# Where the halves of weight chunks land: five places in place of two from the second layer's feed-forward on

## The chip, the cores and the metric

The kernel runs on one core of one Trainium2 chip. The metric is the device time of one execution in microseconds. The kernel before took 1754.6 us (median of 3 runs, 1752.81 to 1756.55). Two runs are told apart here only when they differ by more than about 0.2%, which is 3.5 us.

## The reference

The work is four transformer layers, one after the other, on 256 tokens of width 1024 in f32, with a second stream of 256 context tokens in the first layers.

```python
# layers 0, 1 (first_block)
x = x + g1 * (concat([out_a, out_b, out_c]) @ w_out[i])       # three mixers
x = x + g2 * conv_ffn(modulate(rms_norm(x, n2g), sh2, sc2), w_up[i], conv_w[i], conv_b[i], w_down[i])
# layers 2, 3 (second_block): attention, then a pooling mixer
x = x + gate_m * rmsnorm(y, g_post_mix[i])
x = x + gate_f * rmsnorm(conv_ffn_2(...), g_post_ffn[i])

def conv_ffn(h, w_up, conv_w, conv_b, w_down):
    a = conv3(h @ w_up) + conv_b          # a depthwise convolution over 3 tokens
    gate, val = split(a)                  # in layers 2, 3 only the gate is convolved
    return (silu(gate) * val) @ w_down    # w_up is 1024 x 5632, w_down 2816 x 1024
```

Shift, scale and gate (the modulation) come from one vector per stream, multiplied with a weight of 1024 x 6144 for each layer.

## The kernel before, in words

Every weight matrix is read once, as a list of chunks of up to 128 x 2048 f32 (1 MB), in the order in which they are used (`make_plan`). A chunk passes through two stages:

- **Raw.** `fetch` (L203) issues its load on SP's queue. Most chunks come as two halves of 512 KB (L222 to L224), each into one of two places of the tag `w`. A chunk for which `roomy` (L198) holds comes whole (L219) into one of the seven large rooms of the tag `x8`; such chunks are about every third one of a feed-forward, and not the first ones of it.
- **Parts.** The same function then splits the chunk, in pieces of 384 columns: ACT rounds it to the upper part (`wh`, L238) and DVE subtracts that from the raw piece (`wl`, L240). A place of `w` is free again when the last `wl` piece of its half is done. The parts stand in two rooms of each of the tags `wh` and `wl`, or, for every third chunk, in `x8`.

`weights` (L246) is called by each unit of work on TensorE. For chunk i it has chunks up to i+2 loaded and up to i+1 split (one more where chunk i+2 is roomy). A feed-forward unit `up` is 48 matmuls in groups of 24: the upper part with both parts of h, and the lower part with the upper one (L285, L286, L289). Then ACT and DVE take the result out of PSUM (the tag S, two places): L988, L991 and L993 are the convolution, L1021 the silu, L1024 and L1026 the product, L1028 and L1029 its parts. A unit `down` ends on DVE in L980 (layer 1) or L1051 (layers 2 and 3).

TensorE's instructions and SP's DMA issues stand in program order (`manual_schedule`, L1370). SP waits for nothing but a free place, so it runs ahead of TensorE as far as places allow, and each load waits behind all those ahead of it. ACT's and DVE's instructions are put in order at build time by the scheduler, by its own estimate of when each could start and of the places that are free; on the chip each engine then runs its list in that order.

The modulation has its own loads. `mod_load` (L362) takes a chunk either whole into `x8` or as two halves into the three places of the tag `mw` (L372). The second way is used while the mixers of layers 0 and 1 run (`fill_a`, L955); L410 multiplies with them. From layer 1's feed-forward on, modulation loads go into `x8` (L366).

The stages of the profile are: layer 1's feed-forward (about 925 to 1145 us), layer 2's attention (to 1298), its feed-forward (to 1500), layer 3's pooling mixer (to 1548), its feed-forward (to the end).

Of the kernel before, what the change touches and what calls it, by code (L numbers as in the profile page):

```python
# [11 lines left out]
F32 = mybir.dt.float32  # L12
# [7 lines left out]
P = 128  # L20
# [6 lines left out]
CH = 2048  # L27
# [78 lines left out]
class Stack:  # L106
# [25 lines left out]
    def make_plan(self):  # L132
        plan = []

        def add(name, off, n, extra, cut=None):
            plan.append((name, off, n, extra, cut or n // 2))

        for i in range(4):
            T = 512 if i == 0 else 256
            if i < 2:  # L140
                for c in range(8):
                    add((f"win{i}", c), c * P * CH, CH, False)
                for c in range(4):
                    add((f"wout{i}", c), c * P * CH, CH, c > 1)
                if i == 1:
                    add(("wqkv/c", 0), 0, CH, True)
            elif i == 2:
                for c in range(6):
                    add(("wqkv", c), c * P * CH, CH, False)
                for c in range(4):  # L150
                    add(("wo", c), c * P * CH, CH, True)
            else:
                add(("wpool", 0), 0, CH, True)
            cols = 512 if T == 512 else 256
            off = 0
            for kind, g, j in self.ffn_order(T):
                gk = FF_GROUPS[T][g]
                if kind == "up":
                    add((f"wup{i}", j), j * P * CH, CH, True)
                else:  # L160
                    for c in range(D // cols):
                        add((f"wdn{i}", g, c), off, gk * cols, True, (gk + 1) // 2 * cols)
                        off += P * gk * cols
            if i == 1:
                add(("wqkv/c", 1), P * CH, CH, True)
        base = 1
        for n, (name, off, size, extra, cut) in enumerate(plan):
            if name[0][:3] == "wup" and name[1] == 0:
                base = n + 2
            elif n == 0 or name == ("wo", 0):  # L170
                base = 1 if n == 0 else n + 1
            plan[n] = name, off, size, extra and (n - base) % 3 == 0, cut
        self.plan = plan
        self.early = {}
        n = [p[0] for p in plan].index(("wup2", 0))
        self.early[n - 2] = self.early[n - 1] = n + 1
        self.pos = {p[0]: i for i, p in enumerate(plan)}
        self.raws, self.parts, self.n_whole = [], [], 0

    @staticmethod  # L180
    def ffn_order(T):
# [16 lines left out]
    def roomy(self, n):  # L198
        name, _, _, extra, _ = self.plan[n]
        return (extra and name[0][:3] in ("wup", "wdn") and int(name[0][3]) >= 1 and  # L200
                (name[1] >= 3 if name[0][:3] == "wup" else name[1] < 2))

    def fetch(self, raws, parts):  # L203


        while len(self.raws) < min(raws, len(self.plan)):
            i = len(self.raws)
            (key, *_), off, n, _, c = self.plan[i]
            src = self.a[key.split("/")[0]][off:off + P * n].rearrange("(p n) -> p n", p=P)
            if key in WHOLE:  # L210
                self.n_whole += 1
                w = self.wp.tile([P, CH], F32, tag=("wh", "wl")[self.n_whole % 2], name="ww")
                self.nc.sync.dma_start(out=w[:, :n], in_=src)
                self.raws.append(w)
                continue
            halves = []
            if self.roomy(i):
                w = self.x8("w")
                self.nc.sync.dma_start(out=w[:, :n], in_=src)  # L219
                self.raws.append([w[:, :c], w[:, c:]])  # L220
                continue
            for a, b in ((0, c), (c, n)):  # L222
                w = self.wp.tile([P, CH // 2], F32, tag="w", name="w", bufs=2)
                self.nc.sync.dma_start(out=w[:, :b - a], in_=src[:, a:b])  # L224
                halves.append(w)
            self.raws.append(halves)
        while len(self.parts) < min(parts, len(self.plan)):
            i = len(self.parts)
            (key, *_), _, n, _, c = self.plan[i]
            if key in WHOLE:  # L230
                self.parts.append((self.raws[i],))
                self.raws[i] = None
                continue
            h, l = self.wtile("wh", i), self.wtile("wl", i)
            for (a, b), w in zip(((0, c), (c, n)), self.raws[i]):
                for c in range(a, b, SPLIT):
                    d = min(b, c + SPLIT)
                    self.nc.scalar.copy(h[:, c:d], w[:, c - a:d - a])  # L238
                    with self.tc.issue_after(self.gate[0]) if self.gate and self.gate[1] == 0 else nullcontext():
                        self.nc.vector.tensor_tensor(l[:, c:d], w[:, c - a:d - a], h[:, c:d].bitcast(F32), ALU.subtract)  # L240
            if self.gate:
                self.gate = (self.gate[0], self.gate[1] - 1) if self.gate[1] else None
            self.raws[i] = None
            self.parts.append((h, l))
# [1378 lines left out]
```

## Time and profile before

| | |
|---|---|
| median of 3 runs | 1754.6 us |
| the profiled execution | 1753.49 us, span 1751.7 us, mean granted TensorE clock 0.966 |
| TensorE matmul busy | 1603.6 us (92% of the span), x12604 |
| TensorE weight loads busy | 1419.0 us (81%) |
| DVE busy | 1191.0 us (68%) |
| ACT busy | 880.2 us (50%) |
| DMA | 288.36 MB, mean 165 GB/s |
| chain that ended last | PE 65%, DVE 18%, DMA 8%, ACT 6% |

Busy shares are means over stages with different limits. Lines of TensorE's timeline carry in brackets the idle time ahead of an instruction and what ended it. A matmul is shown with a duration of 0.28 us at the full clock, and such matmuls follow each other at 0.12 us, because they overlap.

### The profile page before, as it was taken

What the parts mean: (1) busy time and instruction counts of PE and PEld (TensorE: products, weight loads), DVE (VectorE), ACT (ScalarE), POOL (GpSimd) and SP (SyncE); (2) the same over time, 40 slices, a digit from 0 to 9 for tenths busy, and PEclk for the clock granted to TensorE, in tenths of its full rate; (3) what the DMA queues carried; (4) which work ended last, traced back from release to release, by engine and by line L of the source; (5) the groups of instructions that cost most, each with busy time, mean ns of one, the idle gap of its engine ahead of it and who ended that gap; (6) DMA issues with size and microseconds to landing.
All of it is one profiled execution on the core that took longest, in us unless ns stands there. A gap on an engine that the chain in (4) does not pass through costs nothing.

```text
span 1751.7 us, 32328 instructions
## 1 busy us (share of the span) xinstructions
PE 1603.6 (92%) x12604; PEld 1419.0 (81%) x12604; DVE 1191.0 (68%) x2879; ACT 880.2 (50%) x2145; POOL 131.6 (8%) x160
## 2 busy tenths in 40 slices
PE   7999887999999999889789899988979999779997
PEld 5878456989898989787468899976759999579996
DVE  5865786755554645787788778785676567876665
ACT  5443644533243423455646656563556565656663
POOL 0000000000000000010000101000141012330110
PEclk9999798999999999999999999998989999889999
DMA  8344331345545454434434454565545546435552
GB/s 312 121 145 145 125 96 61 145 152 191 225 152 221 152 189 168 168 121 132 148 119 145 177 190 140 175 213 209 196 174 172 194 162 225 176 118 198 169 178 88
DMA packets 67403, 288.36 MB, mean 165 GB/s; under 512 B 7729, under 2 KB 9009, under 8 KB 54961
## 3 DMA queue, kind: packets, MB, share of 16 engines
q1 hardware_dynamic: 65664, 283.91, 46.0%
q10 hardware_dynamic: 1584, 2.38, 0.5%
q8 instruction: 99, 1.62, 0.4%
q14 instruction: 56, 0.45, 0.1%
HBM read 285.21 MB, written 1.05 MB: 163 GB/s over the span
## 4 chain that ended last, share of the span: by engine, by line
PE 65%; DVE 18%; DMA 8%; ACT 6%; issue 2%; POOL 0%; SPq 0%; ACTq 0%; DVEq 0%; POOLq 0%
PE S L285 10%; PE S L286 10%; PE S L289 9%; PE acc L285 9%; PE acc L286 8%; PE acc L289 8%; DVE wl L240 5%; PE acc L410 3%; DMA w<-in_wup_dram 3%; ACT wh L238 2%; DMA w<-in_wdn_dram 2%; DVE ht L529 2%; DVE mx L661 1%; PE tr L671 1%; DMA wm<-in_wmod_dram 1%
## 5 line engine op out<-in xcount | busy, mean ns | idle before, releaser
L240 DVE TENSOR_TENSOR wl<-w,wh 128x384 fp32r<-128x384 f32 (+2 forms) x1010 | 489.9, 524 | 216.3 <-ACT wh L238 204.6
L238 ACT CAST wh<-w 128x384 fp32r<-128x384 f32 (+2 forms) x1010 | 422.3, 477 | 323.1 <-DMA w<-in_wup_dram 86.2
L285 PE MATMUL S<-hH,wh 128*128 128x256 f32 x1408 | 351.0, 286 | 28.5 <-ACT hH L539 17.4
L286 PE MATMUL S<-hL,wh 128*128 128x256 f32 x1408 | 349.1, 285 | 4.7 <-POOL hL L537 4.0
L285 PEld LDWEIGHTS S<-hH,wh 128*128 128x128 f32 x1408 | 271.6, 193 | 33.8 <-ACT hH L539 18.1
L286 PEld LDWEIGHTS S<-hL,wh 128*128 128x128 f32 x1408 | 271.4, 193 | 7.1 <-POOL hL L537 5.0
L285 PE MATMUL acc<-gH,wh 128*128 128x256 f32 (+1 forms) x728 | 208.8, 311 | 8.4 <-DVE xc L980 4.8
L286 PE MATMUL acc<-gL,wh 128*128 128x256 f32 (+1 forms) x728 | 205.3, 306 | 0.0
L289 PE MATMUL S<-hH,wl 128*128 128x256 f32 x1408 | 198.3, 284 | 0.0
L289 PEld LDWEIGHTS S<-hH,wl 128*128 128x128 f32 x1408 | 182.5, 193 | 0.0
L285 PEld LDWEIGHTS acc<-gH,wh 128*128 128x128 f32 x728 | 138.8, 191 | 22.5 <-issue 7.5
L289 PE MATMUL acc<-gH,wl 128*128 128x256 f32 (+1 forms) x728 | 145.6, 306 | 0.0
L286 PEld LDWEIGHTS acc<-gL,wh 128*128 128x128 f32 x728 | 138.9, 191 | 5.5
L991 DVE SCALAR_TENSOR_TENSOR cgv<-S,sm,cgv 128x255 f32<-128x255 f32 (+1 forms) x132 | 74.9, 568 | 67.6 <-ACT cgv L988 66.8
L289 PEld LDWEIGHTS acc<-gH,wl 128*128 128x128 f32 x728 | 110.1, 191 | 6.5
L988 ACT ACTIVATE cgv<-S,sm 128x256 f32<-128x256 f32 (+1 forms) x132 | 83.1, 630 | 47.7 <-PE S L289 47.6
L285 PE MATMUL acc<-wh,hH 128*128 128x256 f32 x344 | 90.6, 295 | 10.1 <-ACT hH L539 7.9
L1029 POOL TENSOR_TENSOR gL<-cgv,gH 128x256 fp32r<-128x256 f32 x66 | 52.2, 791 | 573.9 <-ACT gH L1028 552.7
L980 DVE SCALAR_TENSOR_TENSOR x<-acc,mod,x 128x256 f32<-128x256 f32 x104 | 50.0, 482 | 56.8 <-PE acc L289 56.3
L286 PE MATMUL acc<-wl,hH 128*128 128x256 f32 x344 | 87.5, 286 | 0.0
L286 PE MATMUL S<-hcL,wh 128*128 128x256 f32 x352 | 86.5, 284 | 0.3 <-DVE hcL L540 0.3
L285 PE MATMUL S<-hcH,wh 128*128 128x256 f32 x352 | 86.4, 281 | 0.0
(268 smaller groups left out, 2839.0 us busy)
## 6 DMA issues: line engine op xcount, KB each, us to landing
wm<-in_wmod_dram SPq DMA_DIRECT2D x72, 1024.0 KB, 7.6
w<-in_wup_dram SPq DMA_DIRECT2D x140, 512.0 KB, 4.0
w<-in_wdn_dram SPq DMA_DIRECT2D x56, 512.0 KB, 4.0
mw<-in_wmod_dram SPq DMA_DIRECT2D x48, 512.0 KB, 4.6
w<-in_wup_dram SPq DMA_DIRECT2D x18, 1024.0 KB, 7.1
w<-in_win_dram SPq DMA_DIRECT2D x32, 512.0 KB, 4.1
w<-in_wout_dram SPq DMA_DIRECT2D x16, 512.0 KB, 4.8
w<-in_wqkv_dram SPq DMA_DIRECT2D x16, 512.0 KB, 3.8
```

The source lines that it names most:

```text
L238: self.nc.scalar.copy(h[:, c:d], w[:, c - a:d - a])
L240: self.nc.vector.tensor_tensor(l[:, c:d], w[:, c - a:d - a], h[:, c:d].bitcast(F32), ALU.subtract)
L285: mm(o, lhsT=s[0], rhs=m[0], start=k == ks[0], stop=False)
L286: mm(o, lhsT=s[0], rhs=m[1], start=False, stop=False)
L289: mm(o, lhsT=S(b, k)[1], rhs=M(b, k)[0], start=False, stop=end and k == ks[-1])
L410: nc.tensor.matmul(acc[32 * u:32 * u + 32], lhsT=self.cpad[:, k], rhs=w[:, 256 * u:256 * u + 256], start=k == ks[0], stop=k == ks[-1])
L529: nc.vector.scalar_tensor_tensor(t, self.xs[s][:, ft], A, r, ALU.mult, ALU.mult)
L661: nc.vector.tensor_reduce(mx, S[:, :, :nk], AX.X, ALU.max)
L980: self.nc.vector.scalar_tensor_tensor(x, acc[:, c], self.mods(i, j)[:, ft, s:s + 1], x, ALU.mult, ALU.add)
L988: nc.scalar.activation(out, ps, AF.Identity, scale=cw[:, n + f:n + f + 1], bias=cb[:, f:f + 1])
L991: nc.vector.scalar_tensor_tensor(o[:, :, 1:256], x[:, :, 0:255], cw[:, f:f + 1], o[:, :, 1:256], ALU.mult, ALU.add)
L1029: (nc.vector if T == 512 else nc.gpsimd).tensor_tensor(gL[:, a], c[:, 1, :T], gH[:, a].bitcast(F32), ALU.subtract)
```

## The change

From the chunk `("wup1", 0)` on, the halves go in turn into five places: two of the tag `w`, and three of the tag `mw`, in the order mw, w, mw, mw, w. Earlier halves go to `w` as before. Nothing else is edited: which chunks are loaded whole, the order of the loads on SP, the number of rooms for the parts and the memory in use stay as they are.

```diff
-        self.raws, self.parts, self.n_whole = [], [], 0
+        self.raws, self.parts, self.n_whole, self.n_half = [], [], 0, 0
...
+    def raw_half(self, n):
+
+        self.n_half += n >= self.pos["wup1", 0]
+        if self.n_half % 5 in (0, 2):
+            return self.wp.tile([P, CH // 2], F32, tag="w", name="w", bufs=2)
+        return self.mp.tile([P, 1024], F32, tag="mw", name="w", bufs=3)
...
             for a, b in ((0, c), (c, n)):
-                w = self.wp.tile([P, CH // 2], F32, tag="w", name="w", bufs=2)
+                w = self.raw_half(i)
                 self.nc.sync.dma_start(out=w[:, :b - a], in_=src[:, a:b])
```

## Rows read from the trace of the kernel before

**Rows 1.** View by stretches, three feed-forwards; busy us and count by engine, clock, DMA share, GB/s

```profile
925.00:1145.00 220.00, 207.02 (x1677) 203.61 (x1676) 170.06 (x385) 130.29 (x320) 18.79 (x22) 0.98 0.50 168
...
1298.00:1500.00 202.00, 193.72 (x1628) 188.62 (x1628) 133.79 (x300) 119.21 (x293) 34.33 (x44) 0.99 0.56 191
...
1548.00:1742.00 194.00, 189.35 (x1573) 187.89 (x1572) 119.97 (x277) 113.73 (x274) 17.92 (x25) 1.00 0.48 163
```

**Rows 2.** What TensorE waited for, 925 to 1100: total us, times, longest us

```profile
PE S L285 <- DVE cgv L993: 4.8, 7, 1.5
PE S L285 <- ACT wh L238: 4.1, 2, 3.6
PE acc L285 <- DVE x L980: 1.9, 1, 1.9
```

**Rows 3.** What SP's queue waited for, 920 to 1145

```profile
SPq L224 <- DVE wl L240: 159.3, 50, 17.9
...
SPq L219 <- PE S L286: 0.6, 2, 0.3
```

**Rows 4.** SP's timeline at the start of layer 1's feed-forward: start us, us, issue

```profile
905.24 0.33 SPq L224 DMA_DIRECT2D w<-in_wup_dram  x1
...
925.01 14.67 SPq L224 DMA_DIRECT2D w<-in_wup_dram  x4
```

**Rows 5.** Chain of waits, 925 to 975: start us, us, what

```profile
937.41 3.81 DMA w<-in_wup_dram
...
953.53 4.74 DMA w<-in_wup_dram
```

**Rows 6.** TensorE's timeline, 961 to 978: start us, us, instruction, count, idle before

```profile
961.86 1.12 PE L289 MATMUL S<-hH,wl 128*128 128x256 f32 x8
966.56 0.55 PE L285 MATMUL S<-hH,wh 128*128 128x256 f32 x1 [3.58 <-ACT wh L238]
...
971.82 0.41 PE L285 MATMUL S<-hH,wh 128*128 128x256 f32 x1
...
974.83 0.28 PE L285 MATMUL S<-hH,wh 128*128 128x256 f32 x1
```

**Rows 7.** TensorE's timeline, last use of a modulation place in the mixers

```profile
905.08 1.07 PE L410 MATMUL acc<-mw,cpad 128*32 128x256 f32 x16
```

**Rows 8.** Chain of waits, 975 to 1150

```profile
1060.02 8.57 DMA w<-in_wup_dram
```

**Rows 9.** DVE's timeline, 974 to 1003

```profile
980.82 2.39 DVE L240 TENSOR_TENSOR wl<-w,wh 128x384 fp32r<-128x384 f32 x5 [0.42 <-ACT wh L238]
```

**Rows 10.** TensorE's timeline, the wait behind that row

```profile
987.13 0.35 PE L285 MATMUL S<-hH,wh 128*128 128x256 f32 x1 [0.62 <-DVE cgv L993]
```

**Rows 11.** What TensorE waited for, layers 2 and 3's feed-forwards

```profile
PE acc L285 <- DVE y L1051: 1.4, 3, 0.6
PE S L285 <- DVE cgv L1026: 0.9, 1, 0.9
...
PE S L285 <- DVE cgv L1026: 1.0, 1, 1.0
```

**Rows 12.** SP's timeline in layer 2's attention

```profile
1172.70 1.60 SPq L224 DMA_DIRECT2D w<-in_wqkv_dram  x2
1174.35 4.49 SPq L366 DMA_DIRECT2D wm<-in_wmod_dram  x4
```

**Rows 13.** TensorE's timeline in the same place

```profile
1182.68 1.07 PE L410 MATMUL acc<-wm,cpad 128*32 128x256 f32 x16 [1.88 <-DMA wm<-in_wmod_dram]
1185.09 1.94 PE L410 MATMUL acc<-wm,cpad 128*32 128x256 f32 x16 [1.34 <-DMA wm<-in_wmod_dram]
```

**Rows 14.** View by stretches around it, TensorE alone

```profile
1185.00:1195.00 10.00, 9.60 (x66) 0.72 1.01 417
```

**Rows 15.** ACT's timeline at the end of the attention

```profile
1276.49 0.51 ACT L238 CAST wh<-w 128x384 fp32r<-128x384 f32 x1 [2.03 <-DMA w<-in_wup_dram]
```

**Rows 16.** DMA issues of the page: KB each, median us from issue to landing

```profile
w<-in_wup_dram SPq DMA_DIRECT2D x140, 512.0 KB, 4.0
```

## The prediction

> **What bounds the kernel now.** I read the view by stretches first, to see which stage has anything to give. In the three feed-forwards that the change reaches, matmuls fill 207.0 of 220, 193.7 of 202 and 189.4 of 194 us at a clock of 0.98 to 1.00 [rows 1]. So TensorE is the bound there, and only its gaps can be won. [...]
>
> Next, the waits of TensorE, because they say who makes the gaps. In layer 1's feed-forward it waits 4.1 us for ACT's split (longest 3.6), 4.8 us in seven waits for the convolution to free a place of S, and 1.9 us for DVE's update of x [rows 2]. Layers 2 and 3 have only 1.4, 0.9 and 1.0 us of this kind [rows 11].
>
> Then SP's queue, to see why a split is late. SP stands 159.3 us of this stage in front of L224 until a `wl` piece frees a half's place, and only 0.6 us in front of L219 for a large room [rows 3]. Loads are held up by the two places, not by `x8` or by the DMA engines (busy share 0.50 [rows 1]). Last the chain: at the start of the stage it runs from a load to a split to the next load, over and over [rows 5].
>
> **Part A, the start of layer 1's feed-forward.** The chunks up 0 to up 4 are not roomy, so ten halves in a row go through two places. The second half is issued at 905.24, the next only at 925.01, when the first split has freed a place [rows 4]. From there each half costs a landing of 3.8 to 4.7 us and a split before the place is free again [rows 5]. Up 5, which is roomy, is queued behind all ten. TensorE is done with up 4 at 962.98 and starts up 5 at 966.56, after 3.58 idle [rows 6].
>
> With five places, half n waits for half n-5. The three `mw` places were last read by the matmuls that end at 905.08 + 1.07 = 906.15 [rows 7], so this new wait is over before anyone needs the data. Behind it on SP stand only further halves of the same layer, since the loads of the mixers come earlier in the order. Five halves are 2.6 MB; at even 168 GB/s, the mean of the stage [rows 1], they take 15.6 us and have landed near 922, before the first split frees anything (925.01 [rows 4]). The last of ten halves then waits for the fifth half's split, not the eighth's. Three halves are 1.5 chunks, and a chunk is 48 matmuls at 0.12 us, 5.76: both it and up 5 move about 8.6 us forward. That covers 3.58 us.
>
> The gap also cost clock. The first 24 matmuls behind it take from 966.56 to 971.82, 5.26 us, the next 24 to 974.83, 3.01 [rows 6]; at 0.12 us each, the spacing at 2.4 GHz, 24 take 2.88. Lost: 2.4 + 0.1 = 2.5 us. The other wait for a split is 4.1 - 3.6 = 0.5 us [rows 2]. A is 3.6 + 2.5 + 0.5 = **6.6 us**, and I take it whole: 8.6 is over twice the gap.
>
> **Part B, the waits for PSUM and for x in the rest of that stage.** They have two origins. One is a late large load: SP can issue it only behind two halves, at 1060.02, and it lands 8.57 us later [rows 8]; ACT, which runs its list in order, stands in front of it while the convolution's pieces behind it grow late, and so does the place of S. More places take that away. The other is a burst: five `wl` pieces in 2.39 us without a wait among them [rows 9], with TensorE's 0.62 us behind them [rows 10]. More places do nothing for it, and may make bursts commoner, as loaded halves are ready together. Bounds: all of 4.8 + 1.9 = 6.7 us [rows 2], or none and 0.62 for every third of 22 chunks, 7 x 0.62 = 4.3 us lost. I take **3.5 us**, about half, as the long waits are of the first kind.
>
> **Part C, layers 2 and 3's feed-forwards.** 1.4 + 0.9 + 1.0 = 3.3 us are open [rows 11]. Bounds 0 and 3.3; I take **1.5**.
>
> **Part D, layer 2's attention.** Four modulation loads stand behind the halves of `wqkv` on SP: the halves are issued at 1172.70, the loads at once behind them at 1174.35 [rows 12]. TensorE waits 1.88 and 1.34 us for them [rows 13], and the clock in the next 10 us is 0.72 [rows 14]. If 1 is 2.4 GHz and 0.5 is 1.2, the half rate held for (1 - 0.72) / 0.5 = 56% of it, and cost half of that, 2.8 us. Halves that wait for the fifth-last place move these loads forward by about a chunk and a half, at the pace of this stage's splits more than the 3.2 us missing. Gain 0 (if the large rooms are not free earlier) to 3.2 + 2.8 = 6.0; I take **3**, as the rooms can't be seen.
>
> **Part E, the handovers between stages.** At the end of the attention ACT stands 2.03 us in front of a half of `wup2` [rows 15], with the norm's rstd behind it. An earlier half removes up to that; but a split that is ready earlier can also be put ahead of the norm's steps on DVE. Bounds: 2.0 gained, or at each of four handovers a whole chunk's six pieces at 2.39 / 5 = 0.48 us [rows 9], 4 x 2.9 = 11.5 lost. I take **0.4 us**, near the seen row.
>
> No work is added: issues, pieces and bytes are as before.
>
> **Sum.** 6.6 + 3.5 + 1.5 + 3 + 0.4 = 15.0 us, from the profiled execution's 1753.49 us (span 1751.7 and 1.8 around it): 1738.5. That execution lies 1.1 below the median of 1754.6, so against the runs I say **1739.5 us**.
>
> **Rivals.**
>
> 1. *Only the start is mended.* A holds, the rest is bursts and DVE's own load (170 of 220 us busy in layer 1 [rows 1]). 1754.6 - 6.6 = **1748**. For it: the 0.62 behind a burst. Against: the load that lands 8.57 us after a late issue.
>
> 2. *Nothing changes.* Halves get places, and SP then stands in front of the large rooms, so loads start as before, **1754.6**. For it: L219 is in the same queue. Against: only 0.6 us of waiting there in layer 1 [rows 3]; only a part of the halves' 159.3 would have to move there, though.
>
> 3. *Slower: the splits move ahead of the critical steps on DVE.* The scheduler sees halves ready sooner and puts their pieces in front of norm and convolution. Its place is the four handovers and layer 1, its price 2.9 us for each handover and 0.62 for each third chunk: 11.5 + 4.3 = 15.8 lost against A's 6.6, **1764**. It decides once the loss outgrows A, which is three handovers of four without any burst (8.6). For it: bursts exist. Against: the same number of rooms for the parts still holds each split back until TensorE has left a chunk.
>
> 4. *More transfers at once make the needed one late.* A single half takes 4.0 us from issue to landing [rows 16]; five, 2.6 MB, at the 417 GB/s of the busiest stretch [rows 14] take 6.3 us until the last, 2.3 more, at four starts of stages: 9.2 lost against 6.6, **1757**. Against: they are issued much earlier, and in order. The Trainium skill (DMA: Bandwidth & Descriptors, Issuing engines are not separate DMA queues) says that all loads share the same 16 engines and interleave, which is the rule behind this rival; the trace agrees that one stretch can fill them, with a share of 1.01 [rows 14].
>
> **Chances.** Forecast 0.57 (its own range 1732 to 1746), rival 1 0.18, rival 2 0.09, rival 3 0.12, rival 4 0.04. About 0.2%, 3.5 us, is what a measurement tells from no change. Faster by more than that: the forecast and rival 1, 0.75, plus 0.01 from milder forms of the others. Within: rival 2, half of rival 4, some of 3: 0.13. Slower: 0.11. All gains at their upper ends give 6.6 + 6.7 + 3.3 + 6.0 + 2.0 = 24.6, 1730; the lower end reaches past rivals 1 and 2, to 1755. This leaves out most of rivals 3 and 4 and a rest above, about 0.2.
>
> **What would show it.** A: in layer 1, five halves issued by about 907, no `ACT wh` wait of TensorE before up 5, and no dip of the clock there. B: fewer than seven waits for L993 in that stage. D: the four modulation loads issued well before 1174 and no `DMA wm` wait on TensorE. C and E: the waits of rows 11 and 15 gone. Wrong would be a chain that still goes from load to split to load there, SP in front of L219 or L366 for tens of microseconds, or norm steps with more `wl` pieces between them than now.

## The result, and the profile after

The changed kernel takes 1731.2 us (median of 4 runs, 1728.5 to 1735.6) against 1755.6 for the kernel before in the same session (4 runs): a ratio of 0.987, 95% interval 0.984 to 0.989. That is 24.4 us less; 15.0 were forecast. The profiled execution took 1731.5 us, with a span of 1729.7. Medians of a few runs are coarser than the 3.5 us named at the start: in a later session 25 runs of the kernel before spread from 1746.4 to 1763.1 us.

To see where the 24.4 us come from, both executions are cut at the same five places in TensorE's timeline: the first matmul of each feed-forward, the first projection of each mixer behind it, and the last transposes. A stage runs from one of these to the next, so a handover's wait counts for the stage in front of it. The first cut itself lies between 923 and 937 us, although the program ahead of it is the same in every run but one (e12). The stages leave this out, so all experiments below are also given this way. They come from one trace for each kernel, and they vary too. Where several runs have the same places and the same order of instructions in a stage, its lengths lie within 0.6 us in layer 1's feed-forward (200.77 to 201.36) and 1.0 us in the feed-forwards behind. In layer 2's attention they go from 141.90 to 145.65 with two places and the order of before (before, e1 and e2), so differences of 2 or 3 us there need a wait that explains them.

| stage, us | before | after | gain | of it idle | of it busy |
|---|---|---|---|---|---|
| layer 1's feed-forward | 215.79 | 200.80 | 15.0 | 10.7 | 4.3 |
| layer 2's attention | 144.53 | 139.14 | 5.4 | 1.9 | 3.5 |
| layer 2's feed-forward | 215.57 | 212.81 | 2.8 | 2.3 | 0.5 |
| layer 3's pool mixer | 36.41 | 36.51 | -0.1 | -0.3 | 0.2 |
| layer 3's feed-forward | 195.65 | 194.22 | 1.4 | 1.4 | 0.1 |
| sum | 807.95 | 783.48 | 24.5 | 16.0 | 8.5 |

The last two columns come from the view by stretches, cut at these times: idle is the length less TensorE's busy time. Four of the five stages, before and then after, all but the pool mixer (start and end, length, then busy us and count of PE, PEld, DVE, ACT and POOL, granted clock, DMA share, GB/s):

```profile
929.56:1145.35 215.79, 202.81 (x1643) 199.45 (x1641) 166.06 (x376) 128.32 (x316) 18.79 (x22) 0.98 0.50 167
1145.35:1289.88 144.53, 122.35 (x935) 96.45 (x933) 101.74 (x249) 72.19 (x181) 22.76 (x28) 0.94 0.57 209
1289.88:1505.45 215.57, 200.51 (x1658) 194.46 (x1659) 147.33 (x328) 125.40 (x308) 41.07 (x50) 0.97 0.55 190
1541.86:1737.51 195.65, 192.45 (x1585) 191.21 (x1586) 123.78 (x284) 115.59 (x279) 21.35 (x26) 0.98 0.47 162
```

```profile
932.28:1133.08 200.80, 198.52 (x1642) 196.53 (x1641) 166.01 (x376) 125.88 (x316) 18.88 (x22) 1.00 0.55 190
1133.08:1272.22 139.14, 118.88 (x934) 94.46 (x932) 102.19 (x253) 72.53 (x184) 23.38 (x28) 0.96 0.56 205
1272.22:1485.03 212.81, 200.03 (x1658) 195.48 (x1658) 146.09 (x324) 122.92 (x305) 41.23 (x50) 0.96 0.54 189
1521.54:1715.76 194.22, 192.37 (x1584) 191.09 (x1585) 125.45 (x284) 114.37 (x279) 20.79 (x26) 0.98 0.45 155
```

The same work stands in each stage: DVE's busy time in layer 1 is 166.06 and 166.01. TensorE waits less, and its equal number of matmuls also takes less time. In layer 1 and in the attention the granted clock is higher with it (0.98 to 1.00 and 0.94 to 0.96); in layer 2's feed-forward it is not (0.97 to 0.96), and there the busy time hardly changes. A third of the gain, 8.5 us, is this second part.

Of the three waits of [rows 2] in layer 1's feed-forward, 10.8 us together, 0.2 is left. This is all that TensorE waited for from 927 to 1102 (us in total, times, longest; line numbers behind the edit are seven higher, so L285 is L292 now and L238 is L245):

```profile
PE tr L627 <- DVE rp L656: 0.8, 1, 0.8
PE S L292 <- ACT hH L546: 0.7, 1, 0.7
PE S L293 <- DVE hL L547: 0.5, 1, 0.5
PE S L292 <- ACT wh L245: 0.2, 1, 0.2
```

SP's queue (start us, us, issue) shows the cause. By 909.8 five halves are on their way, where before there were two, and up 5's whole load goes out at 945.16. Counted from the stage's start that is 12.9 us, against 953.91 - 929.56 = 24.4 before. The last row is of before:

```profile
899.38 0.38 SPq L231 DMA_DIRECT2D w<-in_wup_dram  x1
906.38 3.42 SPq L231 DMA_DIRECT2D w<-in_wup_dram  x4
927.73 17.38 SPq L231 DMA_DIRECT2D w<-in_wup_dram  x5
945.16 0.59 SPq L226 DMA_DIRECT2D w<-in_wup_dram  x1
```

```profile
953.91 0.42 SPq L219 DMA_DIRECT2D w<-in_wup_dram  x1
```

SP still stands in front of the halves' line for most of the stage, and more than before in front of the large rooms (0.6 us in [rows 3]). TensorE does not wait for that: no load stands in its list of waits above.

```profile
SPq L231 <- DVE wl L247: 168.8, 41, 17.9
SPq L226 <- PE S L296: 15.8, 7, 3.4
```

In the attention TensorE waited for the first two of the four modulation loads (3.2 us in [rows 13]). They go out 10.4 us earlier now, counted from the stage's start: the first after 1151.65 - 1133.08 = 18.6 us, where it was 1174.35 - 1145.35 = 29.0 [rows 12]. TensorE does not wait for them, and the next 10 us run at full clock (0.72 in [rows 14]). SP's queue, TensorE, and the stretch:

```profile
1151.65 14.08 SPq L373 DMA_DIRECT2D wm<-in_wmod_dram  x4
```

```profile
1163.41 1.93 PE L417 MATMUL acc<-wm,cpad 128*32 128x256 f32 x32
1167.62 1.93 PE L417 MATMUL acc<-wm,cpad 128*32 128x256 f32 x32
```

```profile
1170.00:1180.00 10.00, 9.32 (x69) 1.00 1.00 399
```

One thing got worse. The wait at the end of the attention, for the normalised input of the next feed-forward, was 8.3 us and is now 10.28. TensorE before and after:

```profile
1289.88 0.58 PE L285 MATMUL S<-hH,wh 128*128 128x256 f32 x1 [8.32 <-ACT hH L539]
```

```profile
1272.22 0.58 PE L292 MATMUL S<-hH,wh 128*128 128x256 f32 x1 [10.28 <-ACT hH L546]
```

The time goes to pieces of `wl` (L247) on DVE, at two places. Most of it is one piece in front of L1126, which adds up what the norm needs. The piece stands ahead of it in DVE's list and waits for its cast on ACT, and that cast has waited 1.03 us for a half of `wup2`. So L1126 starts 1264.63 - 1261.94 = 2.69 us after the wait began; before (L1119) it was 1282.61 - 1281.56 = 1.05. This is 1.6 of the 2.0 us. From there to the end of L511 it takes 6.20 us, with pieces between the norm's steps (L509 to L511), where it was 5.88: the other 0.3. DVE before, then DVE and ACT after:

```profile
1282.61 0.83 DVE L1119 TENSOR_TENSOR sx<-sx,m 128x256 f32<-128x256 f32 x1
```

```profile
1262.07 0.95 DVE L1125 TENSOR_TENSOR m<-m,rstd 128x256 f32<-128x256 f32 x1
1263.94 0.77 DVE L247 TENSOR_TENSOR wl<-w,wh 128x384 fp32r<-128x384 f32 x1 [0.91 <-ACT wh L245]
1264.63 0.94 DVE L1126 TENSOR_TENSOR sx<-sx,m 128x256 f32<-128x256 f32 x1
...
1269.29 0.41 DVE L247 TENSOR_TENSOR wl<-w,wh 128x256 fp32r<-128x256 f32 x1
1269.62 0.41 DVE L510 TENSOR_TENSOR var<-var,rstd 128x256 f32<-128x256 f32 x1
1269.96 0.55 DVE L247 TENSOR_TENSOR wl<-w,wh 128x384 fp32r<-128x384 f32 x1
1270.42 0.41 DVE L511 SCALAR_TENSOR_TENSOR rstd<-var,rstd 128x256 f32<-128x256 f32 x1
```

```profile
1263.39 1.23 ACT L245 CAST wh<-w 128x384 fp32r<-128x384 f32 x3 [1.03 <-DMA w<-in_wup_dram]
```

This leads to a second difference between the two kernels. The order of instructions on SP and on TensorE is the same in both, but the order on ACT and on DVE is not: it is set by a scheduler that reckons when each half will be ready. In the traces the two lists differ from layer 1's feed-forward on and in no place before it. So the change is two changes, more places and a new order, and the experiments take them apart.

### The profile page after: what moved, and what is told of

Read it like the earlier page. It is cut to its first block, busy times and chain, and to the rows that moved or that the text cites. A ratio compares the mean times of both kernels' runs of the same rounds, so it can differ in the third digit from the quotient of the medians.

```text
span 1729.7 us, 32332 instructions
## 1 busy us (share of the span) xinstructions
PE 1598.9 (92%) x12604; PEld 1416.6 (82%) x12604; DVE 1192.2 (69%) x2879; ACT 873.5 (51%) x2145; POOL 131.9 (8%) x160
## 3 DMA queue, kind: packets, MB, share of 16 engines
HBM read 285.21 MB, written 1.05 MB: 165 GB/s over the span
## 5 line engine op out<-in xcount | busy, mean ns | idle before, releaser
L247 DVE TENSOR_TENSOR wl<-w,wh 128x384 fp32r<-128x384 f32 (+2 forms) x1010 | 491.0, 526 | 171.5 <-ACT wh L245 146.4
L245 ACT CAST wh<-w 128x384 fp32r<-128x384 f32 (+2 forms) x1010 | 414.6, 475 | 245.1 <-PE acc L417 76.3
L292 PE MATMUL S<-hH,wh 128*128 128x256 f32 x1408 | 349.2, 285 | 20.9 <-ACT hH L546 19.8
L292 PEld LDWEIGHTS S<-hH,wh 128*128 128x128 f32 x1408 | 271.1, 193 | 24.7 <-ACT hH L546 20.5
L292 PE MATMUL acc<-gH,wh 128*128 128x256 f32 (+1 forms) x728 | 208.4, 310 | 5.8 <-DVE xc L987 4.8
L292 PEld LDWEIGHTS acc<-gH,wh 128*128 128x128 f32 x728 | 139.1, 191 | 19.0 <-issue 8.1
L998 DVE SCALAR_TENSOR_TENSOR cgv<-S,sm,cgv 128x255 f32<-128x255 f32 (+1 forms) x132 | 74.7, 566 | 72.6 <-ACT cgv L995 72.4
L995 ACT ACTIVATE cgv<-S,sm 128x256 f32<-128x256 f32 (+1 forms) x132 | 83.0, 629 | 56.0 <-PE S L296 55.9
L292 PE MATMUL acc<-wh,hH 128*128 128x256 f32 x344 | 90.3, 294 | 10.3 <-ACT hH L546 8.1
L1035 ACT CAST gH<-cgv 128x256 fp32r<-128x256 f32 (+1 forms) x88 | 40.5, 460 | 92.1 <-DVE cgv L1031 70.8
```

Of the source, the lines that this page charges most:

```text
L292: mm(o, lhsT=s[0], rhs=m[0], start=k == ks[0], stop=False)
L995: nc.scalar.activation(out, ps, AF.Identity, scale=cw[:, n + f:n + f + 1], bias=cb[:, f:f + 1])
L998: nc.vector.scalar_tensor_tensor(o[:, :, 1:256], x[:, :, 0:255], cw[:, f:f + 1], o[:, :, 1:256], ALU.mult, ALU.add)
L1035: nc.scalar.copy(gH[:, a], c[:, 1, :T])
```

## The experiments

All times are us. The ratio is to the kernel before in the same session (medians 1754.5 to 1756.0). The column "stages" is the sum of the five stages above (807.95 before, 783.48 after); the pool mixer, 36.40 to 36.52 in every run, has no column of its own.

| run | median | ratio to before, 95% | layer 1 | attention | layer 2 ff | layer 3 ff | stages |
|---|---|---|---|---|---|---|---|
| e1, five places in layer 1's ff only | 1740.4 | 0.992 (0.990 to 0.995) | 200.77 | 145.65 | 215.49 | 195.57 | 793.90 |
| e2, first ten halves only | 1743.7 | 0.994 (0.992 to 0.996) | 206.98 | 141.90 | 216.09 | 196.56 | 797.95 |
| e3, from the attention on | 1745.6 | 0.995 (0.993 to 0.997) | 216.18 | 138.08 | 212.36 | 194.46 | 797.60 |
| e4, five places, order of before | 1735.3 | 0.990 (0.985 to 0.995) | 208.55 | 135.67 | 213.12 | 194.25 | 787.98 |
| e5, three places | 1726.0 | 0.985 (0.983 to 0.987) | 199.96 | 137.93 | 212.05 | 194.23 | 780.68 |
| e6, four places | 1732.2 | 0.989 (0.986 to 0.991) | 203.31 | 138.81 | 214.00 | 194.73 | 787.35 |
| e7, five places, gate at a norm | 1730.3 | 0.987 (0.985 to 0.990) | 200.82 | 135.64 | 213.00 | 194.22 | 780.19 |
| e8, order of before in the attention | 1730.3 | 0.986 (0.984 to 0.989) | 201.36 | 138.15 | 212.12 | 194.23 | 782.37 |
| e9, three places, order of before | 1739.6 | 0.990 (0.987 to 0.994) | 206.61 | 138.90 | 213.45 | 194.23 | 789.61 |
| e10, five places, order of e5 | 1727.2 | 0.985 (0.983 to 0.988) | 199.98 | 136.43 | 211.79 | 194.22 | 778.93 |
| e11, three places and the gate | 1725.6 | 0.984 (0.981 to 0.986) | 200.31 | 135.45 | 212.27 | 194.23 | 778.77 |
| e12, e11 from layer 0's ff on | 1723.9 | 0.982 (0.980 to 0.985) | 201.40 | 135.49 | 215.88 | 194.29 | 783.56 |

**Where the gain is made: e1, e2, e3.** The same five places, but only for a part of the halves.

e1:

```diff
-        self.n_half += n >= self.pos["wup1", 0]
+        if not self.pos["wup1", 0] <= n < self.pos["wqkv/c", 1]:
+            return self.wp.tile([P, CH // 2], F32, tag="w", name="w", bufs=2)
+        self.n_half += 1
```

> The five places only for the chunks of layer 1's feed-forward; from layer 2's attention on two places again. Theory 1 (each stage gains by its own earlier loads): the stretch from the first matmul of layer 1's feed-forward to the first one of layer 2's attention stays at the 199 to 200 us of the changed kernel (214.4 before), the later stages go back to their old lengths (143.7 from there to layer 2's feed-forward, 215.6, 36.4, 196.8), and the whole gains 15 us. Theory 2 (the gain is one shift that is handed on, the later stages gain because layer 1 leaves earlier): most of the 24 us remain.

e2, the ten halves of up 0 to up 4 alone, against e1:

```diff
-        if not self.pos["wup1", 0] <= n < self.pos["wqkv/c", 1]:
+        if not self.pos["wup1", 0] <= n <= self.pos["wup1", 4]:
```

> The five places only for the ten halves of up 0 to up 4 of layer 1's feed-forward. Theory 1 with the prediction's part A: the split's wait of 3.58 us, the half clock behind it and the 0.5 us wait go, 6.6 us in all, and the seven waits for a place of S and the one for x (6.7 us) stay as they were. Theory 3 (the whole of layer 1's gain comes from its start, since a stage that starts with loaded halves stays ahead to its end): 13 to 15 us.

e3, all but layer 1's:

```diff
-        self.n_half += n >= self.pos["wup1", 0]
+        self.n_half += n >= self.pos["wqkv/c", 1]
```

> The five places only from the second chunk of wqkv/c on, so layer 1's feed-forward is as before. Theory 1: layer 1's stretch is back at 214 us, the later four stretches keep their new lengths (138.3, 212.8, 36.5, 195.4), and the whole gains 9 to 10 us. Theory 2: next to nothing is gained.

e1 gains 14.1 in its stages, all of it in layer 1's feed-forward (15.0 there; the attention loses 1.1). e3 gains 10.4, all of it behind that. Together 24.4, against 24.5 for the change: each stage earns its own, and neither part needs the other. The medians say the same (14.9 and 9.7 us, 10 runs each). In e2 layer 1 gains 8.8 of its 15.0. The rest is made later in the stage, where e2 still waits 3.5 us for the convolution, four times (L294 is e2's L292). Its attention is 2.6 us shorter although nothing in it is edited, and TensorE waits no less for the modulation loads there than before; this is no gain of the places.

```profile
PE S L294 <- DVE cgv L1002: 3.5, 4, 1.4
PE tr L629 <- DVE rp L658: 0.8, 1, 0.8
```

**Places or order: e4.** The change, with every instruction of ACT, DVE and POOL held to the order that it has in the kernel before. The lists are copied from there, and each entry depends on the one ahead of it, which adds no wait between engines.

```diff
...
+def pin(tc):
+    by = {i.name: i for i in tc.nc.cur_bb.bb.instructions}
+    for seq in ORDER.values():
+        seq = [f"I-{n}" for n in seq.split() if f"I-{n}" in by]
+        for p, q in zip(seq, seq[1:]):
+            tc.add_manual_dep(by[q], p, mybir.DependencyInfo(mybir.DependencyClass.NoSync, mybir.DependencyReason.DATA),
+                              reason="pin")
...
+    pin(tc)
```

> Five places as in the changed kernel, but ACT's, DVE's and GpSimd's instructions pinned to the order that they have in the kernel before; nothing else differs. Theory 1 (loads that start earlier on the chip): at least 18 of the 24 us stay, TensorE's 3.58 us wait for the split is gone, and ACT's waits for loads of w_up in the three feed-forwards fall from 55 us to under 15. Theory 4 (the scheduler's new order of ACT and DVE is what gains): under 6 us are gained, as the old lists keep the splits where they stood.

The places alone are worth 20.0 of the 24.5: 7.2 in layer 1, 8.9 in the attention, 2.5 and 1.4 in the feed-forwards behind. The new order adds 4.5, and that is a difference of two effects: it wins 7.8 in layer 1 (208.55 to 200.80) and loses 3.5 in the attention (135.67 to 139.14). The first is far beyond what layer 1 varies by: four runs with the new order there take 200.77 to 201.36, two with places and the old order 206.61 and 208.55. Of the second, the 2.0 us in the handover's wait are firm (10.28 and 10.29 in the change and e3, 8.32 or 8.33 in the five runs with the order of before); the other 1.5 are within what the attention varies by. The medians (1735.3 and 1731.2) can't tell e4 from the change. The reverse, two places with the new order, has no run.

The places do what they were meant to: with the order held, ACT's waits for loads of `w_up` in the three feed-forwards fall from 54.7 us to none.

e4 also shows what the new order does in layer 1. Its loads are as early as the prediction said: up 5's is issued 938.81 - 923.11 = 15.7 us after the stage's start, 8.7 less than before. Yet by the labels of the rows TensorE still waits 2.7 us for a split, and 1.9 for x. TensorE's waits, SP's issue, and TensorE at the place:

```profile
PE S L292 <- ACT wh L245: 2.7, 1, 2.7
PE acc L292 <- DVE x L987: 1.9, 1, 1.9
...
PE S L292 <- DVE cgv L1000: 0.6, 1, 0.6
```

```profile
938.81 0.43 SPq L226 DMA_DIRECT2D w<-in_wup_dram  x1
```

```profile
958.39 0.35 PE L292 MATMUL S<-hH,wh 128*128 128x256 f32 x1 [2.70 <-ACT wh L245]
...
962.81 0.28 PE L292 MATMUL S<-hH,wh 128*128 128x256 f32 x1
```

The clock dips behind it as before: 24 matmuls take 962.81 - 958.39 = 4.42 us. ACT's and DVE's timelines at that place:

```profile
953.58 0.42 ACT L1028 ACTIVATE cgv<-cgv 128x256 f32<-128x256 f32 x1 [2.01 <-DVE cgv L1000]
953.90 2.35 ACT L245 CAST wh<-w 128x384 fp32r<-128x384 f32 x6
956.16 1.01 ACT L995 ACTIVATE cgv<-S,sm 128x256 f32<-128x256 f32 x2
957.07 2.05 ACT L245 CAST wh<-w 128x384 fp32r<-128x384 f32 x5
```

```profile
954.43 2.64 DVE L247 TENSOR_TENSOR wl<-w,wh 128x384 fp32r<-128x384 f32 x6 [0.95 <-ACT wh L245]
956.98 0.87 DVE L998 SCALAR_TENSOR_TENSOR cgv<-S,sm,cgv 128x255 f32<-128x255 f32 x2
957.77 0.86 DVE L1000 SCALAR_TENSOR_TENSOR cgv<-S,sm,cgv 128x255 f32<-128x255 f32 x2
```

The profile puts the wait down to a split, but this cannot be the one that up 5 needs. By the program's lists the six casts of 953.90 are up 5's, over at 956.25, and the five of 957.07 are up 6's. The matmul that starts up 5 waits for two things, a split and a place of S, and S has two places: up 5 needs the one of up 3. That place is free when L1000 has read its second half, the first of the two of 957.77, which is over at about 958.24; TensorE starts at 958.39. It is late because of up 5's own split: the second half's L995 stands behind six casts on ACT, and its L998 and L1000 stand behind six pieces of `wl` in one block of 2.64 us on DVE. The kernel before has the same block at the same place, with the same lag: its L993 pair starts at 965.94, the first is over at about 966.4, and TensorE starts at 966.56 [rows 6]. In e9, which has this order too, it is again 2.67 us. In e3, where this stage has the places and the order of before, it is 4.81, so the step from 3.58 to 2.70 is no sign that places shorten it.

The new order puts up 5's casts ahead of the silu of up 2, about a chunk earlier. They are over at 954.41, 10.8 us before TensorE starts up 5 (965.18), and no block of them stands on ACT between the two halves of an evacuation. On DVE three pieces of `wl` in a row (1.35 us from 956.17) are the most between two halves there. ACT of the changed kernel:

```profile
951.73 2.06 ACT L245 CAST wh<-w 128x384 fp32r<-128x384 f32 x5 [0.45 <-DMA w<-in_wup_dram]
...
954.00 0.41 ACT L245 CAST wh<-w 128x256 fp32r<-128x256 f32 x1
954.31 0.56 ACT L995 ACTIVATE cgv<-S,sm 128x256 f32<-128x256 f32 x1
956.34 0.42 ACT L1028 ACTIVATE cgv<-cgv 128x256 f32<-128x256 f32 x1 [1.47 <-DVE cgv L1000]
956.66 0.55 ACT L995 ACTIVATE cgv<-S,sm 128x256 f32<-128x256 f32 x1
```

That the order is what removes this wait is shown (same places, e4 against the change). That it is the place of S and not a split can be read from the trace of e4. TensorE waits for DVE in an instruction of its own, ahead of the weight load, and that instruction is released at 958.28, 0.03 us after the update of the first of the two L1000 (958.25). The matmul starts 0.11 us later. Before and in e9 the same two steps take 0.03 and 0.11 us (966.43, 966.46, 966.56 and 971.83, 971.86, 971.96). In e11 the same matmul stalls for 0.24 us, again with 0.03 and 0.11, and there ACT updates nothing in the 0.2 us ahead of it. The instruction in e4:

```profile
L292 PEldq EVENT_SEMAPHORE  x1: 51/51/51, 958.3 to 958.3; - x1
```

**How many places: e5 and e6.** In e5 two halves of three go to `w` and wait for the third-last one's split; every third goes to `mw`, whose three places are more than it needs:

```diff
-        if self.n_half % 5 in (0, 2):
+        if self.n_half == 0 or self.n_half % 3:
```

> Three places in place of five from layer 1's feed-forward on: w, w, mw in turn, so a half waits for the third-last one's split. By the prediction's rule a place moves a load half a chunk, 2.9 us, forward. Theory 1: the 3.58 us wait in layer 1 shrinks but does not go, layer 1's stretch lies between, at 204 to 211 us (215.8 with two, 200.8 with five places), the attention at 140 to 143, and the whole gains 8 to 16 us. Rival: any place beyond two lets the scheduler order the splits well, and 21 to 25 us are gained.

e6, `mw` and `w` by turns, so that a half in `w` waits for the fourth-last one's split:

```diff
-        if self.n_half % 5 in (0, 2):
+        if self.n_half % 2 == 0:
```

> Four places' worth: w and mw by turns, so a half in w waits for the fourth-last one's split (mw has a place to spare). Theory 1: 5.8 us forward covers the 3.58 us wait, layer 1's stretch is 200 to 204 us, and the whole gains 19 to 25 us, so the fifth place is worth under 4 us. Rival (each further place counts alike): 16 us.

Three places gain 27.3 in the stages, not the 8 to 16 that I had expected, and more than the 21 to 25 of the rival named beside them. Four gain 20.6, within the 19 to 25 expected; five gain 24.5. A gain that falls and rises again with the number of places is not one of depth alone, so the order was the suspect again.

**Depth with the order held equal: e9 and e10.** e9 is e5 with `pin` and the order of before, to be set beside e4. e10 is the change with `pin` and the order of e5. For e9, with ORDER as in e4:

```diff
-        if self.n_half % 5 in (0, 2):
+        if self.n_half == 0 or self.n_half % 3:
...
+    pin(tc)
```

> Three places, and ACT's, DVE's and GpSimd's instructions pinned to the order of the kernel before. Lists equal, only the number of places differs from the run with five places and the old lists (208.6, 135.7, 213.1, 36.4, 194.3 in the five stretches). If the places beyond the third do nothing on the chip, every stretch is within 1 us of these. If depth counts there, layer 1's stretch is at 210 to 214 and the attention's at 138 to 142.

For e10, with ORDER from e5:

```diff
...
+    pin(tc)
```

> Five places, with the order of ACT, DVE and GpSimd that the scheduler made for three places. If the lists set the rest of the difference, the stretches are those of the run with three places (200.0, 137.9, 212.1, 36.5, 194.2) within 1 us. If more places help a list on the chip, layer 1 or the attention is shorter by over 1 us.

With the order of before, three places give 789.61 and five 787.98. With e5's order they give 780.68 and 778.93. So the fourth and fifth place are worth 1.6 to 1.8 us in either order, and the third has the rest of what places bring: 807.95 - 789.61 = 18.3 of 20.0. With three places and the order of before, too, ACT waits for no load of `w_up` in the three feed-forwards. The 1.6 to 1.8 us are no more than what stages vary by; what speaks for them is a wait. What five gain on three lies in the attention (3.2 us between e9 and e4, less 1.9 in layer 1, where e9 was shorter, against both of the outcomes named for it). There three places leave a wait for a modulation load, 1.21 us in e9 and 1.09 in e5, that e4 and e10 do not have. Of e9:

```profile
1180.64 1.07 PE L417 MATMUL acc<-wm,cpad 128*32 128x256 f32 x16 [1.21 <-DMA wm<-in_wmod_dram]
```

Between the orders, at five places: 787.98, 783.48 and 778.93. That spread, 9.1 us, is over five times what the depth is worth.

**The handover: e7 and e8.** Two ways to keep the new pieces away from the norm. e7 orders the `wl` pieces of the next split behind the norm's rstd at the end of the attention, by a gate that the kernel already sets at another norm. e8 holds only the instructions of the attention and its handover to the order of before.

```diff
+        if (i, j) == (2, 3):
+            self.gate = ir.ins, 0
```

> The changed kernel, and the subtractions of one chunk of w_up of layer 2 queued on DVE behind the last step of the rstd at the attention's end, as the kernel already does at layer 3's feed-forward. If the pieces of wl between the norm's steps make the 10.28 us wait of TensorE there (8.32 before), the wait falls to 8.0 to 8.6 us, the stretch from layer 2's attention to its feed-forward from 139.1 to 136 to 137.5 us, the others stay, and the whole is 2 us below the changed kernel. If the wait is the chain of the norm's own steps, it stays at 10.3.

e8, with these stages' instructions alone in ORDER:

```diff
...
+    pin(tc)
```

> The changed kernel, with ACT's, DVE's and GpSimd's instructions of layer 2's attention and its handover (and those alone) pinned to the order of the kernel before. If the orders act stage by stage, layer 1's stretch keeps the 200.8 us of the new order, the attention's takes the 135.7 that five places had with the old lists, the later ones stay at 212.8, 36.5 and 194.2, and the whole gains 27 to 28 us on the kernel before, 3.5 more than the changed kernel. If the attention's 135.7 hangs on what layer 1 leaves behind, it stays at 138 to 139.

The wait is 10.28 us after the change, 8.33 in e4, 8.04 in e7 and 9.28 in e8. Of e7 and e8, TensorE's timeline:

```profile
1271.76 0.58 PE L292 MATMUL S<-hH,wh 128*128 128x256 f32 x1 [8.04 <-ACT hH L546]
```

```profile
1272.18 0.58 PE L292 MATMUL S<-hH,wh 128*128 128x256 f32 x1 [9.28 <-ACT hH L546]
```

In e7 DVE has no `wl` piece from 1261.9 to the end of the norm, and L1126 starts 0.8 us after the wait began, where it was 2.69. e7's attention takes 135.64, e4's 135.67: the 3.5 us that the new order lost there come back with one edge. Two waits of TensorE at the stage's end have 3.0 of it: 10.28 to 8.04, and 1.32 to 0.54 for `msum` just ahead. It shows in the stages (3.3 us less) but not in the medians (1730.3 and 1731.2). e8 was a miss. I expected the attention at about 135.7; it took 138.15, and of the handover's 2.0 us only 1.0 came back. The order of before inside the stage did not give its time where what surrounds it is ordered anew; why is not shown.

**Two versions put together: e11 and e12.** e11 is three places and the gate; e12 is e11 with the places from layer 0's feed-forward on, its diff against e11.

```diff
-        if self.n_half % 5 in (0, 2):
+        if self.n_half == 0 or self.n_half % 3:
...
+        if (i, j) == (2, 3):
+            self.gate = ir.ins, 0
```

> Three places, and the subtractions of one chunk of layer 2's w_up queued behind the norm's rstd as in the run with the gate. If the two add, the attention's stretch falls from 137.9 to about 135 and the five stretches sum to 777 to 779 us, against 783.5 of the changed kernel; the median is then 2 to 3 us under that of the run with three places, about the 0.2% that can be told.

```diff
-        self.n_half += n >= self.pos["wup1", 0]
+        self.n_half += n >= self.pos["wup0", 0]
```

> As the run before, with the turns through three places begun at layer 0's feed-forward, so that the mixers' modulation loads of layer 1 share their places with halves. If TensorE's waits at the start of layer 1's mixers (3.71 us for a split) go, the time before layer 1's feed-forward shrinks by 3 to 5 us. If sharing makes halves wait for modulation matmuls, the mixers get longer by that or more. The five stretches after it stay within 3 us of the run before.

e11 has the attention of e7 (135.45) and the rest of e5, 778.77, the shortest stages of all and level with e10. By the medians it is not told from e5 (1725.6 and 1726.0). e12 has the lowest median, 1723.9, by 1.7 us, again too little to be told apart, and loses 3.6 us in layer 2's feed-forward, so that its stages are 4.8 us longer than e11's, where at most 3 were expected. What its earlier places should have removed, the split that TensorE waits for at the start of layer 1's mixers, is still there:

```profile
758.76 0.36 PE L292 MATMUL acc<-wh,hcH 128*128 128x256 f32 x1 [3.71 <-ACT wh L245]
```

Both medians lie below the changed kernel's, by 5.6 and 7.3 us. For e11 the stages show 4.7 of it. For e12 they show none (783.56 against 783.48), so its lead lies ahead of the first cut, where runs differ anyway.

## Why the prediction was right, and where it was off

The direction, and places as its main cause, were right. The size was low by 9.4 us: 1731.2 lies just below the forecast's own range (1732 to 1746) and inside the wide one (1730 to 1755). That the sum of all upper ends, 24.6, meets the measured 24.4 is chance: parts C and D and the clock gave more than their upper ends, part E cost time, and 4.5 of the 24.5 us in the stages come from the new order, which the prediction had only as a loss. By steps:

- **Part A** (6.6 at the start of layer 1). The forward shift was 8.6 by the prediction and 8.7 in e4. The step that failed is "I take it whole: 8.6 is over twice the gap". It took the 3.58 us for a wait on a split, as the row's label has it, and so for a late load. With the loads 8.7 earlier and the order of before, 2.70 of it stays, and e4's trace shows TensorE released by the place of S, which is late behind a block of up 5's split. The term came true because the scheduler also moved that split, which is luck as far as the prediction goes.
- **Part B** (3.5 of a possible 6.7). This is a size that was off. All of 6.7 went: the idle time of the stage fell by 10.7, against A's 3.6 + 0.5 and B's 6.7, 10.8 together. "About half, as the long waits are of the first kind" was too careful about the bursts; with the order made for five places they cost TensorE no wait for a place of S at all. With the order of before, 0.6 of 4.8 and all of the 1.9 for x stay, and A's 2.70 is of this kind too.
- **The clock.** The prediction put 2.5 us on it in layer 1, only behind the one long gap; the busy time fell by 4.3.
- **Part C** (1.5 of 3.3). Layers 2 and 3 gave 2.8 + 1.4 = 4.2, a little over the upper end. In e4, with places alone, it was 2.5 + 1.4. The waits of [rows 11] went from 3.3 to 1.0; the 0.9 and the 1.0 for the gate's product (L1026) are gone. The rest came from waits that the sum did not have, such as those for hL in layer 3 (2.2 to 0.7).
- **Part D** (3 of 6.0). Also too low. The 3.2 us of waits and the dip of the clock are gone, and busy time fell by 3.5, where 2.8 was the upper end. e4 gains 8.9 in the stage, with the handover as before. The forward shift of the first two loads was 10.4 us.
- **Part E** (0.4, between 2.0 and -11.5). The sign was wrong: the handover behind the attention lost 2.0 in its wait, 1.6 of it by one piece of `wl` that waits for its cast and so for a load, and 0.3 by the pieces between the norm's steps. By e4 and e7 the new order costs 3.5 in that stage.

**The rivals.** Rival 1 falls: e2 mends little but the start and gains 10.0 in the stages (2.6 of them in the attention, where it edits nothing), the change 24.5. Rival 2 named a wait that did come, 15.8 us in front of a large room, without effect on TensorE. Rival 3 is real in part: splits do stand ahead of the norm's steps, and e7 takes them out again. But the costly one is a piece that waits for its own cast, not the 0.48 us of a piece itself. One handover lost 2.0 us in its wait, the two behind it 0.2 and 0.4, and layer 1 lost nothing. What I did not see is that the same mechanism wins elsewhere; there the new order is worth 7.8. Rival 4 falls: with the DMA engines at a share of 1.00 and 399 GB/s between 1170 and 1180, TensorE waits for no load in the attention.

The Trainium skill (Perfetto Trace Analysis, Identifying the Most-Contended Engine) calls the busy share of matmuls no good measure of how close TensorE is to its roofline and names that of the weight loads in its place. By the weight loads of [rows 1] some 36 us were open in those three stretches. The three feed-forwards gained 15.0 + 2.8 + 1.4 = 19.2, so the traces agree as far as a ceiling can.

**Still open.** The value of the new order with two places, why the attention varies by up to 3.7 us with the same places and order, and why the order made for four places is worse than those for three and five (787.35 against 780.68 and 783.48). By e9 and e10 the depth cannot be the reason, but no run held four places to another order.

## What to carry to other kernels

When a buffer gets deeper under a scheduler that orders instructions by when it reckons data to be ready, count two changes: the loads that move, and the lists that are made anew. Holding the lists to the old order shows the first alone: here 20.0 of 24.5 us, 18.3 of them from the third place, while the new list moved single stages by -3.5 to +7.8. Where an instruction waits for two things, look up in the lists and in the trace's own wait instruction which of them was last, before a wait is priced by its label. And where a piece of work is put ahead of a critical step, ask what that piece waits for: here 0.77 us of work cost 1.6.

## What was not expected of the hardware

- The gain in idle time came with a gain in clock. In layer 1 and the attention TensorE's idle time fell by 12.6 us and its busy time, for the same matmuls, by another 7.8, at a granted clock of 1.00 and 0.96 where it had been 0.98 and 0.94. e4 kept the 2.70 us stall, and there layer 1 stays at 0.98 and its busy time falls by 1.6 us in place of 4.3.
- The four modulation loads now take 14.08 us to be issued (4.49 in [rows 12]): SP stands 12.0 us in front of the third until TensorE has left a place, so the last two go out only 0.8 us earlier in the stage than before. The stage is shorter for all that, as TensorE had waited for the first two.
